# Row sums over single squares: the norm behind a down projection, with some of its additions moved to TensorE

## The chip, the cores and the metric

The kernel runs on one core of a Trainium2 chip. The metric is device time in microseconds (us). The kernel before took 2602.65 us, the median of three runs (2602.61 to 2605.37).

The engines are TensorE (PE; the profile shows its matmuls as PE and its weight loads as PEld), VectorE (DVE), ScalarE (ACT), GpSimd (POOL) and SyncE (SP), which here only issues DMAs. PE multiplies a stationary 128x128 block with a moving block and writes into PSUM banks of 512 float32 columns; DVE and ACT read the banks.

## The reference, cut to what matters

Two layers of a diffusion backbone run over 1024 latent tokens of width 1024, with a context of 256 tokens in front. Layer 0 mixes tokens by retention, layer 1 by a short gated convolution; each mixer is followed by a SwiGLU feed-forward network (FFN). Every sub-layer starts with an RMS norm over the 1024 features of a token, then a shift and a scale:

```
def rms_norm(x, gain=None):
    y = x * rsqrt(mean(x * x, axis=-1) + EPS)
    return y * gain

hx = hx + g1 * mixer(modulate(rms_norm(hx, norm_mix), sh1, sc1))
hx = hx + g2 * swiglu(modulate(rms_norm(hx, norm_ffn), sh2, sc2))
...
return rms_norm(hx, final_norm)
```

So four times a projection ends, a gated result is added to the residual stream, and the next thing that is needed is, per token, the sum of the squares of all 1024 features: after the retention output projection, after the first FFN, after the convolution's output projection and after the second FFN, where the norm makes the kernel's output.

## The kernel before, in words

The stream is held with features on partitions: eight tiles `H[kt, tb]` (kt 0 to 7) of 128 features by 512 tokens for each of the two halves of the tokens (tb). Matrix products are done in float32 by splitting both operands into a high and a low part: three matmuls for each block, in `mm3` (lines 160 to 162, the bulk of PE's work). The operands are made by a cast on ACT (L155, L150) and a subtraction on DVE (L156, L151). Large products use a Winograd-like scheme of seven sub-products, numbered 1 to 7, over a two by two division.

`down` (called four times) is the down projection. Its loop goes over sub-products in the order 1, 5, 6, 3, 7, 4, 2. Sub-products 3 and 7 finish the four upper and 4 and 2 the lower half of the work; 4 and 2 belong to the token half `order[0]`, 4 first (kt 4 to 7), then 2 (kt 0 to 3). For a finished tile, `finished` calls `update` (L1267: PSUM times gate plus residual, on DVE), and `complete`: ACT squares the tile, and `sq_add` (square L294, add L298 on DVE) adds the square to one running tile `accs[tb]`. ACT also stores the tile to DRAM (L1290) in the first three calls.

The last rows of sub-product 2 are done column by column (c = 0 to 3), so that tiles become final one after the other: over four rows in the retention output projection and the first FFN, over two rows in the convolution (`short`, with four rows in all). In the last call the tokens of sub-product 2 are also split in two (`LATER`), and the second 256 tokens come at the very end, one column after the other.

The norm follows as steps. `rstd` sums the squares over the partitions on PE: for each block of 128 tokens (j) the running tile is the stationary operand and one column of ones moves (L303); this leaves the sum of each token on its partition, one column of a PSUM bank for each block. Then come a scaling (L308) and an inverse square root by Newton steps, all small DVE operations (L166 to L178). `rstd_diag` puts the result on four diagonals (L321), and `spread` multiplies ones with them (L329), which makes a bank with the factor of each token in all partitions; the modulators (L1445 and ACT L1447, L1449) apply it, and what they give are operands of the next layer. The first sub-products of the next layer only need the other token half, whose norm runs during sub-product 2.

At the end of the kernel there is no spread: the finished tiles are scaled by the final gain (L1559), transposed on PE into banks of 128 tokens by 512 features (`result_turn`, L1553), and `result_end` multiplies each bank by the factor of its tokens, even banks on DVE (L1574), odd ones on ACT (L1572), and sends each piece of 256 KB out by a DMA on SP's queue (L1575). Feature half e = 1 goes first, then e = 0.

The order of the work on each engine is not the written one everywhere. Steps of the next layer are written between products by a list of hooks, and a planner in the framework then orders the instructions of each engine ahead of the run: of those that its own cost model has ready, the one written first. Two accesses to one PSUM bank stand in a fixed order wherever the planner sees a dependence. Tiles come from pools with a fixed number of buffers: `ttile` has 12, PSUM has 8 banks.

Of the kernel before, what the change touches and what calls it, by code (L numbers as in the profile page):

```python
# [14 lines left out]
AF = mybir.ActivationFunctionType  # L15
ALU = mybir.AluOpType

P = 128
# [3 lines left out]
TB = 512  # L22
# [30 lines left out]
def hybrid_kernel(ctx: ExitStack, tc: tile.TileContext, a: dict):  # L53
    nc = tc.nc
# [18 lines left out]
    def ttile():  # L73
        return tp.tile([P, 512], F32, tag="t", name="tt")
# [15 lines left out]
    def bank():  # L90
        return pp.tile([P, 512], F32, tag="p", name="ps")
# [32 lines left out]
    ones = const.tile([P, P], F32, name="ones")  # L124
# [4 lines left out]
    hooks = deque()  # L129
# [106 lines left out]
    def until(ready):  # L236
        while not ready():
            hooks.popleft()()
# [53 lines left out]
    def sq_add(acc, h, first, n=512, eng=nc.vector):  # L292
        s = acc if first else ttile()
        ins = nc.scalar.activation(s[:, :n], h, AF.Square)  # L294
        if eng is nc.gpsimd:
            tc.keep_in_program_order(ins)
        if not first:
            eng.tensor_tensor(acc[:, :n], acc[:, :n], s[:, :n], op=ALU.add)  # L298

    def rstd(acc, nb, ps):  # L300

        for j in range(nb):
            nc.tensor.matmul(  # L303
                ps[:, j : j + 1], acc[:, j * P : (j + 1) * P], ones[:, 0:1],
                start=True, stop=True,
            )
        v = sm.tile([P, 8], F32, tag="rs_v", name="rs_v")
        nc.vector.tensor_scalar(  # L308
            v[:, :nb], ps[:, :nb], 1.0 / D, EPS, op0=ALU.mult, op1=ALU.add
        )  # L310
        y = sm.tile([P, 8], F32, tag="rs_y", name="rs_y")
        rsqrt(y[:, :nb], v[:, :nb], nb)
        return y

    def rstd_diag(acc, n):

        nb = n // P
        y = rstd(acc, nb, bank())
        dg = ttile()
        for j in range(nb):  # L320
            nc.vector.tensor_scalar(  # L321
                dg[:, j * P : (j + 1) * P], ident, y[:, j : j + 1], None, op0=ALU.mult
            )
        return dg

    def spread(dg, n):

        rb = bank()
        nc.tensor.matmul(rb[:, :n], ones, dg[:, :n], start=True, stop=True)  # L329
        return rb  # L330
# [230 lines left out]
    acc = ttile()  # L561
# [4 lines left out]
    dg = rstd_diag(acc, CTX)  # L566
# [596 lines left out]
    last = 2 * len(T_ORDER) - 1  # L1163
# [27 lines left out]
    LATER = slice(0, TB // 2), slice(TB // 2, TB)  # L1191
# [4 lines left out]
    def down(src, nh, w, gate, residual, order, consume, then=(), last=False):  # L1196
# [3 lines left out]


        seq = [(n, i) for n in (1, 5, 6, 3, 7, 4, 2) for i in range(nh)]
        wr, ws, xl, xs, accs, made = {}, {}, {}, {}, {}, set()

        def w_load(k, half):
            if k not in wr:
# [59 lines left out]
                h, ps = H[kt, tb][:, t], ps[:, t]  # L1266
                nc.vector.scalar_tensor_tensor(h, ps, g, h, op0=ALU.mult, op1=ALU.add)  # L1267

        def norm_steps(tb):
            box = {}  # L1270

            def diag():
                box["dg"] = rstd_diag(accs[tb], TB)

            def bank_of(i, step):
                if i == 0:
                    box["rb"] = spread(box["dg"], TB)
                step(box["rb"])

            return [diag, nothing] + [lambda i=i, f=f: bank_of(i, f) for i, f in enumerate(consume(tb))]  # L1280

        def complete(kt, tb, t):
            h = H[kt, tb]
            if tb not in accs:
                accs[tb] = ttile()
                nc.scalar.activation(accs[tb], h, AF.Square)
            else:
                sq_add(accs[tb][:, t], h[:, t], False, t.stop - t.start)
            if not last:
                nc.scalar.dma_start(h_d[kt][tb], h)  # L1290

# [6 lines left out]
        short = nh == KT // 2  # L1298
# [8 lines left out]
        def step(ps, c, w, x, t, first, end):  # L1307
            k = slice(c * P, (c + 1) * P)
            mm3(ps[:, t], w[:, 0, k], w[:, 1, k], x[:, 0, t], x[:, 1, t], first, end, False)

        def run():
            banks, kept = {}, []
            by_column = 0 if last else min(4, nh // 2)

            def finished(n, c, ps, t):
                j, r = D_OUT[n]
                kt, tb = 4 * j + c, order[r]
                update(n, kt, tb, ps, t)
                if n in (3, 7, 2, 4):
                    complete(kt, tb, t)  # L1320
                if last and n in (2, 4):
                    result_tile(kt, t)

            for m, (n, i) in enumerate(seq):
                which = "A" if n in (1, 6, 7, 4) else "B"
                if i == 0:
                    if n == 7:
                        load_h()
                    if n == 5:
                        until(lambda: src(2, nh - 1) is not None)  # L1330
                    if n in (1, 5, 2):
                        banks[which] = [bank() for _ in range(4)]
                    if n == 4:
                        hooks.extend(then[:1])
                        hooks.extend(norm_steps(order[1]))
                        hooks.extend(then[1:])
                    if n == 2 and last:
                        hooks.extend(
                            lambda kt=kt: result_turn(kt, LATER[0]) for kt in range(4, KT)
                        )  # L1340
                if n == 1 and not short:
                    w_rest(i)
                if n == 6:
                    w_load(nh + i, 0)
                until(lambda: m in ws)
                operands(m + D_AHEAD)
                w, x = ws.pop(m), xs.pop(m)
                if n == 2 and i == nh - by_column - 1:
                    operands(m + D_AHEAD + 1)
                if n == 2 and i >= nh - by_column:  # L1350
                    kept.append((i, w, x))
                    if i < nh - 1:
                        continue
                    for c in range(4):
                        ps = banks[which][c]
                        for k, w, x in kept:
                            step(ps, c, w, x, TOKENS, k == 0, k == nh - 1)
                        finished(n, c, ps, TOKENS)
                        unit_done(2)
                    continue  # L1360
                t = TOKENS
                if last and n == 2:
                    kept.append((w, x))
                    t = LATER[0]
                for c in range(4):
                    step(banks[which][c], c, w, x, t, n in (1, 5, 2) and i == 0, i == nh - 1)
                if i == nh - 1:
                    for c in range(4):
                        finished(n, c, banks[which][c], t)
                unit_done(2 if n in (1, 2, 4) or nh == 4 else 1)  # L1370
            if last:
                flush()
                acc = accs[order[0]]
                for c in range(4):
                    ps = bank()
                    for i, (w, x) in enumerate(kept):
                        step(ps, c, w, x, LATER[1], i == 0, i == nh - 1)
                    finished(2, c, ps, LATER[1])
                    if c == 0:
                        for kt in range(4):  # L1380
                            result_turn(kt, LATER[0])
                        y = result_norm(acc, LATER[0])
                    if c == 1:
                        result_end(y, LATER[0])
                        for kt in range(4, KT):
                            result_turn(kt, LATER[1])
                    if c > 1:
                        result_turn(c - 2, LATER[1])
                y = result_norm(acc, LATER[1])
                for c in (2, 3):  # L1390
                    result_turn(c, LATER[1])
                result_end(y, LATER[1])
            else:
                hooks.extend(norm_steps(order[0]))

        return ahead, run

# [160 lines left out]
        h = H[kt, 1][:, t]  # L1558
        nc.scalar.activation(h, h, AF.Copy, scale=cols[:, C_FIN + kt : C_FIN + kt + 1])  # L1559

    def result_norm(acc, t):
        return rstd(acc[:, t], (t.stop - t.start) // P, bank())

    def result_end(y, t):

        t0 = t.start // P
        for e in (1, 0):
            for tt in range(t0, t.stop // P):
                r = ttile()
                ps, f = r_banks.pop((tt, e)), y[:, tt - t0 : tt - t0 + 1]  # L1570
                if tt % 2:
                    nc.scalar.activation(r, ps, AF.Copy, scale=f)  # L1572
                else:
                    nc.vector.tensor_scalar(r, ps, f, None, op0=ALU.mult)  # L1574
                nc.sync.dma_start(a["out"][tt * P : (tt + 1) * P, e * 512 : (e + 1) * 512], r)  # L1575


    def conv_tap(k, ft):
# [68 lines left out]
    for i, (r, _) in enumerate(seq):  # L1647
# [8 lines left out]
        if r is not None and r[1] == steps - 1:  # L1656
            h = r[0]
# [135 lines left out]
```

## Time and profile before

| what | value |
|---|---|
| median of three runs | 2602.65 us |
| the profiled execution | 2606.16 us |
| its span, first to last instruction | 2604.4 us |
| PE, PEld, DVE, ACT, POOL busy | 98%, 80%, 73%, 48%, 14% |
| mean granted clock of TensorE | 0.994 |
| chain of waits, share of PE | 85% |

The profile shows one execution. A row of a timeline gives start, duration, engine, line, operation, what it writes and reads and how often, and in brackets how long the engine had been idle and for what it waited. A row of the chain of waits gives start, duration and the instruction whose end released the next. A table of windows gives the busy time of PE, PEld, DVE, ACT and POOL in each stretch, with their counts in brackets, then the granted clock, the share of the DMA engines and GB/s.

### The profile page before, as it was taken

What the parts mean: (1) busy time and instruction counts of PE and PEld (TensorE: products, weight loads), DVE (VectorE), ACT (ScalarE), POOL (GpSimd) and SP (SyncE); (2) the same over time, 40 slices, a digit from 0 to 9 for tenths busy, and PEclk for the clock granted to TensorE, in tenths of its full rate; (3) what the DMA queues carried; (4) which work ended last, traced back from release to release, by engine and by line L of the source; (5) the groups of instructions that cost most, each with busy time, mean ns of one, the idle gap of its engine ahead of it and who ended that gap; (6) DMA issues with size and microseconds to landing.
All of it is one profiled execution on the core that took longest, in us unless ns stands there. A gap on an engine that the chain in (4) does not pass through costs nothing.

```text
span 2604.4 us, 33352 instructions
## 1 busy us (share of the span) xinstructions
PE 2552.3 (98%) x11444; PEld 2091.2 (80%) x11444; DVE 1914.1 (73%) x3366; ACT 1248.9 (48%) x2245; POOL 352.4 (14%) x441
## 2 busy tenths in 40 slices
PE   8999999999999999999999999999989999999998
PEld 4788888887777887888888888888768888888888
DVE  7886797765887778777875768877687666656766
ACT  6743333446766555433333545533465333334544
POOL 1102343002211202000002100200112100002100
PEclk9999999999999999999999999999999999999999
DMA  9456344764789946455557855432684333329723
GB/s 355 172 178 238 106 162 166 267 210 163 253 297 301 256 152 144 158 193 163 177 198 240 249 160 153 92 104 88 198 235 97 121 98 109 109 89 318 190 86 114
DMA packets 220106, 466.08 MB, mean 179 GB/s; under 512 B 23841, under 2 KB 53665, under 8 KB 219937
## 3 DMA queue, kind: packets, MB, share of 16 engines
q1 hardware_dynamic: 149808, 307.90, 36.2%
q0 software_dynamic: 39744, 101.74, 14.9%
q10 hardware_dynamic: 30384, 54.32, 5.7%
q8 instruction: 90, 1.47, 0.2%
q14 instruction: 80, 0.65, 0.1%
HBM read 331.22 MB, written 120.06 MB: 173 GB/s over the span
## 4 chain that ended last, share of the span: by engine, by line
PE 85%; DMA 5%; DVE 4%; issue 3%; ACT 2%; POOL 1%; SPq 0%; DVEq 0%; ACTq 0%; POOLq 0%
PE ps L160 28%; PE ps L162 28%; PE ps L161 28%; DVE u L156 2%; DMA raw<-in_ada_w 1%; DMA tt<-os_d 1%; DMA raw<-in_w_o 1%; PE ps L1049 1%; DMA tt<-x_d 1%; DMA u<-q_d 1%; DMA raw<-in_w 0%; ACT u L155 0%; DMA raw<-in_w_kc 0%; DMA t<-h_d 0%; PE ps L329 0%
## 5 line engine op out<-in xcount | busy, mean ns | idle before, releaser
L160 PE MATMUL ps<-u 128*128 128x512 f32 (+1 forms) x3492 | 1362.1, 391 | 18.2 <-DVE u L156 6.7
L161 PE MATMUL ps<-u 128*128 128x512 f32 (+1 forms) x3492 | 1354.5, 388 | 2.7 <-DVE u L156 2.7
L162 PE MATMUL ps<-u 128*128 128x512 f32 (+1 forms) x3492 | 1353.9, 388 | 0.0
L160 PEld LDWEIGHTS ps<-u 128*128 128x128 f32 x3492 | 658.3, 189 | 161.6 <-DVE u L156 6.2
L161 PEld LDWEIGHTS ps<-u 128*128 128x128 f32 x3492 | 658.9, 189 | 137.8 <-DVE u L156 4.4
L162 PEld LDWEIGHTS ps<-u 128*128 128x128 f32 x3492 | 658.5, 189 | 134.7 <-issue 0.7
L155 ACT CAST u<-raw 128x512 fp32r<-128x512 f32 (+1 forms) x634 | 387.6, 627 | 357.4 <-PE ps L162 201.3
L156 DVE TENSOR_TENSOR u<-raw,u 128x512 fp32r<-128x512 f32 (+1 forms) x634 | 451.7, 726 | 46.6 <-ACT u L155 45.4
L156 DVE TENSOR_TENSOR u<-tt,u 128x512 fp32r<-128x512 f32 x328 | 217.5, 686 | 111.4 <-ACT u L155 109.4
L155 ACT CAST u<-tt 128x512 fp32r<-128x512 f32 x328 | 194.6, 620 | 197.3 <-DMA tt<-x_d 85.4
L478 ACT COPY tt<-ps 128x512 f32<-128x512 f32 x192 | 112.8, 587 | 224.6 <-PE ps L162 220.8
L151 DVE SCALAR_TENSOR_TENSOR u<-raw,u 128x512 fp32r<-128x512 f32 x168 | 114.9, 687 | 65.1 <-ACT u L150 65.1
L150 ACT ACTIVATE u<-raw 128x512 fp32r<-128x512 f32 x168 | 105.2, 631 | 81.3 <-PE ps L162 69.6
L1407 POOL DMA_DIRECT2D x_d<-tt x52 | 28.3, 544 | 843.2 <-DVE tt L1420 744.0
L766 DVE SCALAR_TENSOR_TENSOR u<-ps,u 128x512 fp32r<-128x512 f32 x128 | 85.3, 686 | 38.0 <-ACT u L765 37.7
L491 DVE TENSOR_TENSOR tt<-tt,ps 128x512 f32<-128x512 f32 x64 | 43.7, 682 | 71.7 <-PE ps L162 71.7
L765 ACT ACTIVATE u<-ps 128x512 fp32r<-128x512 f32 x128 | 73.8, 598 | 33.6 <-PE ps L162 31.6
L485 DVE TENSOR_TENSOR tt<-tt,ps 128x512 f32<-128x512 f32 x64 | 43.8, 685 | 52.5 <-ACT tt L478 51.9
L1267 DVE SCALAR_TENSOR_TENSOR t<-ps,ada,t 128x512 f32<-128x512 f32 x48 | 33.9, 747 | 51.1 <-PE ps L162 48.2
L156 DVE TENSOR_TENSOR u<-t,u 128x512 fp32r<-128x512 f32 x78 | 52.7, 686 | 19.2 <-ACT u L155 18.6
L224 DVE SCALAR_TENSOR_TENSOR t<-t,c_row 128x512 f32<-128x512 f32 x88 | 57.5, 684 | 9.5 <-DMA t<-in_ada_t 9.5
L708 POOL TENSOR_TENSOR u<-t,u 128x512 fp32r<-128x512 f32 x24 | 32.2, 1344 | 223.4 <-DVE tt L1024 113.0
(184 smaller groups left out, 2132.4 us busy)
## 6 DMA issues: line engine op xcount, KB each, us to landing
raw<-in_w SPq DMA_DIRECT2D x88, 512.0 KB, 4.1
tt<-x_d SPq DMA_DIRECT2D x176, 256.0 KB, 4.0
t<-in_ada_t SPq DMA_DIRECT2D x88, 256.0 KB, 6.5
raw<-in_w SPq DMA_DIRECT2D x88, 256.0 KB, 6.1
x_d<-tt ACTq DMA_DIRECT2D x78, 256.0 KB, 2.6
raw<-in_w_v SPq DMA_DIRECT2D x36, 512.0 KB, 5.1
raw<-in_ada_t SPq DMA_DIRECT2D x36, 512.0 KB, 5.5
x_d<-tt POOLq DMA_DIRECT2D x52, 256.0 KB, 2.7
```

Of the source, the lines that this page charges most:

```text
L150: nc.scalar.activation(dst_hi, src, AF.Copy, scale=-1.0)
L151: nc.vector.scalar_tensor_tensor(dst_lo, src, -1.0, dst_hi.bitcast(F32), op0=ALU.mult, op1=ALU.subtract)
L155: nc.scalar.copy(dst_hi, src)
L156: nc.vector.tensor_sub(dst_lo, src, dst_hi.bitcast(F32))
L160: nc.tensor.matmul(ps, w_hi, x_lo, start=first, stop=False, **kw)
L161: nc.tensor.matmul(ps, w_lo, x_hi, start=False, stop=False, **kw)
L162: nc.tensor.matmul(ps, w_hi, x_hi, start=False, stop=last, **kw)
L224: nc.vector.scalar_tensor_tensor(w[e], w[e], 1.0, c_row[:, k], op0=ALU.mult, op1=ALU.mult, accum_out=sums[:, e, ct : ct + 1],)
L478: nc.scalar.copy(m[p, n], ps)
L485: nc.vector.tensor_add(t, t, banks[p, "c"])
L765: nc.scalar.activation(s[:, 0], st[d][m], AF.Copy, scale=f)
L766: nc.vector.scalar_tensor_tensor(s[:, 1], st[d][m], f, s[:, 0].bitcast(F32), op0=ALU.mult, op1=ALU.subtract,)
```

## The change

In `complete`, for tiles of sub-product 2, the square is no longer added to the running tile but kept in a tile of its own (the list `apart`): for c = 2 and 3 in the retention output projection and the first FFN, for all four c in the convolution, and for c = 3 of the last 256 tokens at the end. `rstd` takes these tiles and adds them up in PSUM: for each block of 128 tokens one matmul for the running tile and one for each tile apart, accumulated into the same column. In `result_end` the e = 1 pieces of the last 256 tokens are scaled and sent in two halves of 256 features.

```
-    def rstd(acc, nb, ps):
+    def rstd(acc, nb, ps, apart=()):
+        terms = [acc, *apart]
         for j in range(nb):
-            nc.tensor.matmul(
-                ps[:, j : j + 1], acc[:, j * P : (j + 1) * P], ones[:, 0:1],
-                start=True, stop=True,
-            )
+            for i, q in enumerate(terms):
+                nc.tensor.matmul(
+                    ps[:, j : j + 1], q[:, j * P : (j + 1) * P], ones[:, 0:1],
+                    start=i == 0, stop=i == len(terms) - 1,
+                )
...
-        def complete(kt, tb, t):
+        def complete(kt, tb, t, alone):
...
-                sq_add(accs[tb][:, t], h[:, t], False, t.stop - t.start)
+                n = t.stop - t.start
+                if alone:
+                    apart.append(ttile())
+                    nc.scalar.activation(apart[-1][:, :n], h[:, t], AF.Square)
+                else:
+                    sq_add(accs[tb][:, t], h[:, t], False, n)
...
                 if n in (3, 7, 2, 4):
-                    complete(kt, tb, t)
+                    alone = n == 2 and t != LATER[0] and c >= (3 if last else 0 if short else 2)
+                    complete(kt, tb, t, alone)
...
-                y = result_norm(acc, LATER[1])
+                y = result_norm(acc, LATER[1], apart)
...
-                hooks.extend(norm_steps(order[0]))
+                hooks.extend(norm_steps(order[0], apart))
...
-                if tt % 2:
-                    nc.scalar.activation(r, ps, AF.Copy, scale=f)
-                else:
-                    nc.vector.tensor_scalar(r, ps, f, None, op0=ALU.mult)
-                nc.sync.dma_start(a["out"][tt * P : (tt + 1) * P, e * 512 : (e + 1) * 512], r)
+                n = 2 if e and t == LATER[1] else 1
+                for k in range(n):
+                    w = slice(k * 512 // n, (k + 1) * 512 // n)
+                    if tt % 2:
+                        nc.scalar.activation(r[:, w], ps[:, w], AF.Copy, scale=f)
+                    else:
+                        nc.vector.tensor_scalar(r[:, w], ps[:, w], f, None, op0=ALU.mult)
+                    nc.sync.dma_start(
+                        a["out"][tt * P : (tt + 1) * P, e * 512 + w.start : e * 512 + w.stop],
+                        r[:, w],
+                    )
```

More of the change, by code (lines that the diff above doesn't have):

```diff
@@ L313, in rstd, with rstd_diag @@
         return y
-    def rstd_diag(acc, n):
+    def rstd_diag(acc, n, apart=()):
         nb = n // P
-        y = rstd(acc, nb, bank())
+        y = rstd(acc, nb, bank(), apart)
         dg = ttile()
@@ L1202, in down @@
         seq = [(n, i) for n in (1, 5, 6, 3, 7, 4, 2) for i in range(nh)]
-        wr, ws, xl, xs, accs, made = {}, {}, {}, {}, {}, set()
+        wr, ws, xl, xs, accs, made, apart = {}, {}, {}, {}, {}, set(), []
         def w_load(k, half):
@@ L1267, in update, with norm_steps @@
                 nc.vector.scalar_tensor_tensor(h, ps, g, h, op0=ALU.mult, op1=ALU.add)
-        def norm_steps(tb):
+        def norm_steps(tb, apart=()):
             box = {}
             def diag():
-                box["dg"] = rstd_diag(accs[tb], TB)
+                box["dg"] = rstd_diag(accs[tb], TB, apart)
             def bank_of(i, step):
@@ L1559, in result_tile, with result_norm @@
         nc.scalar.activation(h, h, AF.Copy, scale=cols[:, C_FIN + kt : C_FIN + kt + 1])
-    def result_norm(acc, t):
-        return rstd(acc[:, t], (t.stop - t.start) // P, bank())
+    def result_norm(acc, t, apart=()):
+        return rstd(acc[:, t], (t.stop - t.start) // P, bank(), apart)
     def result_end(y, t):
```

## The prediction, made before the changed kernel was run

> **What bounds the kernel now.** I read the page first, then the chain of waits at the places where a down projection hands over to what follows, then the busy time and the granted clock of single stretches.
>
> ```profile
> span 2604.4 us, 33352 instructions
> PE 2552.3 (98%) x11444; PEld 2091.2 (80%) x11444; DVE 1914.1 (73%) x3366; ACT 1248.9 (48%) x2245; POOL 352.4 (14%) x441
> ...
> PE 85%; DMA 5%; DVE 4%; issue 3%; ACT 2%; POOL 1%; SPq 0%; DVEq 0%; ACTq 0%; POOLq 0%
> ```
>
> TensorE (PE) is busy 98% of the span and holds 85% of the chain. Work added to PE therefore shows in the end unless it falls into one of PE's few gaps, and work taken from VectorE (DVE) shows only where PE waits for DVE. Those gaps stand at four places that the change touches: the end of the retention output projection (992 us), of the first FFN (1626), of the convolution (1950), and of the kernel (2594). At the first, the chain runs:
>
> ```profile
> 992.49 0.76 DVE tt L1267
> 993.33 0.64 ACT tt L294
> 993.99 0.70 DVE tt L298
> 994.74 1.19 PE ps L303 x8
> 995.93 0.64 PE ps L160
> ```
>
> Update of the last tile, its square, the add on DVE, then the row sums: four matmuls, each of two passes, hence x8. The timeline gives PE's idle time ahead of the sums here and, second, at the convolution:
>
> ```profile
> 994.74 1.19 PE L303 MATMUL ps<-ones,tt 128*128 128x1 f32 x8 [2.29 <-DVE tt L298]
> 1954.15 1.44 PE L303 MATMUL ps<-ones,tt 128*128 128x1 f32 x8 [3.30 <-DVE tt L298]
> ```
>
> So PE does nothing from 992.45, and there from 1950.85, until DVE's add is through. What that costs beside the wait is seen in stretches cut where the clock changes:
>
> ```profile
> 992.10:995.51 3.41, 1.12 (x9) 0.77 (x7) 1.44 (x2) 1.10 (x2) 0.00 (x0) 1.00 0.22 83
> 995.51:998.93 3.42, 3.42 (x11) 2.74 (x11) 2.55 (x16) 0.00 (x0) 0.00 (x0) 0.50 0.00 0
> 998.93:1002.34 3.41, 3.41 (x15) 2.45 (x14) 1.48 (x4) 1.00 (x2) 0.00 (x0) 1.00 0.00 0
> 1626.14:1629.55 3.41, 3.41 (x21) 2.94 (x20) 1.44 (x2) 1.22 (x2) 0.00 (x0) 1.00 0.20 77
> 1944.42:1947.84 3.42, 1.79 (x7) 0.93 (x5) 3.42 (x6) 3.02 (x6) 0.00 (x0) 1.00 0.69 156
> 1951.25:1954.66 3.41, 0.51 (x5) 0.51 (x5) 2.85 (x5) 2.52 (x5) 0.00 (x0) 1.00 0.41 154
> 1954.66:1958.08 3.42, 3.42 (x11) 2.92 (x12) 2.28 (x10) 0.00 (x0) 0.00 (x0) 0.50 0.00 0
> 1958.08:1961.49 3.41, 3.41 (x8) 2.31 (x7) 1.56 (x9) 0.53 (x1) 0.00 (x0) 0.50 0.00 0
> ```
>
> The first number behind the window is its length, the second PE's busy time, the third from the right the granted clock. The clock changes on a grid of 3.41 us: after one with PE busy 1.12 or 0.51 us the next has half the clock, after one with 1.79 us it has not. A half-clock stretch loses up to 1.7 us of PE work. At the convolution there are two in a row, although PE was busy throughout the first of them: the row sums stand at its start, for 0.9 us (until 1955.59, quoted below) as against 0.4 us in the stretch from 995.51 (until 995.93). I read this as: the sums, which move one column each, hardly count as work for the clock. Where the stretches begin relative to the program need not be the same in each run.
>
> **The change, place by place.** The price of a pass, with the clock full, comes from the first FFN's end:
>
> ```profile
> 1628.68 0.95 PE L303 MATMUL ps<-ones,tt 128*128 128x1 f32 x8
> 1629.49 0.49 PE L160 MATMUL ps<-u 128*128 128x512 f32 x1
> ...
> 1632.97 1.13 PE L329 MATMUL ps<-tt,ones 128*128 128x512 f32 x2 [0.46 <-DVE tt L321]
> ```
>
> Eight passes take 1629.49 − 1628.68 = 0.81 us, 0.10 us each; with the clock partly halved they take 1.19 us or 1.44 us (at 994.74 and 1954.15), so up to 0.18 each. With two tiles apart the row sums grow from 8 to 24 passes, with four apart to 40, at the very end from 4 to 8.
>
> No row shows in which order PE will run the new passes. The code writes them column block by column block, and within a block the ready sums first and the last tile's last. All write one bank, and I assume that the planner keeps them as written; then the first block's ready terms run early, but the other blocks' terms stand behind the last square. The bound on the other side, all ready terms run early, is the first rival.
>
> *Retention output projection* (two tiles apart). The last square ends at 993.97, so the sums can go on 0.7 us earlier than 994.74: −0.7. Four of the 24 passes fit into the wait, 20 follow it where 8 did: 12 × 0.10 = +1.2. The two removed adds free DVE, which nobody waits for. From 992.45 on PE now idles or runs sums until about 996.0, 3.5 us; the half clock at 995.51 would slow the last of them (a quarter of the 20 at 0.18 instead of 0.10: +0.4). Sum +0.9; bounds −0.7 (early terms) and +2.6 (one half-clock stretch more).
>
> *First FFN's end.* Here nothing is gained from the removed adds: PE was busy through the whole stretch from 1626.14 to 1629.55 (3.41 of 3.41 us), with the next layer's product until the sums began, so it never waited for L298. The 16 further passes are PE work: +1.6. What can take some of it back is the 0.46 us in which PE waits for the norm's diagonal at 1632.97, if the planner puts the sums into the middle of that product. I take +1.4; bounds +1.1 and +1.8. Twenty passes in a row are 2 us in which the clock may see little work, where 0.81 us did no harm: a half-clock stretch (1.7) with a chance of one in four, +0.4.
>
> *Convolution* (four tiles apart). Here DVE does bound:
>
> ```profile
> L298 DVE TENSOR_TENSOR tt<-tt 128x512 f32<-128x512 f32 x4 | 2.7, 676 | 0.0
> ...
> 1951.03 0.66 DVE tt L1267
> 1951.69 0.60 DVE tt L298
> 1952.82 0.68 DVE u L151
> 1953.50 0.61 DVE tt L298
> 1954.15 1.44 PE ps L303 x8
> 1955.59 0.64 PE ps L160
> ```
>
> All four adds between 1943 and 1954.2 are removed, and DVE has no idle time in front of them (0.0). Two stand ahead of the last update (2 × 0.60 = 1.2 us); from the last square's end (1952.3, one square of 0.64 after the update's 1951.69) to the sums were 1.8 us more. So the last square is there about 3.0 us before 1954.15, near 1951.2. Eight of the 40 passes fit in front of it, 32 follow where 8 did: 24 × 0.10 = +2.4 at full clock, +4.3 at 0.18. Net −0.6 to +1.3; as the clock halves at some point of this long thin stretch, +0.3.
>
> *End of the kernel.* One tile of 256 tokens apart, and the first two output pieces halved.
>
> ```profile
> 2594.57 0.42 ACT tt L294
> 2595.02 0.43 DVE tt L298
> 2595.50 0.62 PE ps L303 x4
> ...
> 2598.50 1.41 DVE L1574 TENSOR_SCALAR tt<-ps,rs_y 128x512 f32<-128x512 f32 x2
> 2599.26 1.79 SPq L1575 DMA_DIRECT2D out<-tt  x4
> ...
> 2601.00:2602.00 1.00, 0.00 (x0) 0.00 (x0) 0.00 (x0) 0.00 (x0) 0.00 (x0) 0.50 1.02 387
> DMA to landing us min/median/max: 2.0/2.4/2.7
> ```
>
> Without the add the sums can start at 2595.03, −0.47; two more passes stand behind the square, +0.2. Half a piece leaves DVE about 0.26 us sooner (an add of 128x256 takes 0.43 in the chain, one of 128x512 0.70), so the first issue falls at 2599.00 and not 2599.26. But SP then issues six times instead of four, 1.79 / 4 = 0.45 us apart: the last at 2599.00 + 5 × 0.45 = 2601.25 instead of 2599.26 + 3 × 0.45 = 2600.6. The DMA engines are full while the pieces go out (share 1.02, 387 GB/s), a 256 KB piece takes 0.68 us, and an unhindered one lands after 2.0 us, 1.3 of them before its data move. The fifth issue (2600.80) then lands at 2602.8 and the sixth 0.68 later, 2603.5; before, the last landed at 2600.6 + 2.7 = 2603.3. So +0.2 from the halves. Sum −0.1; bounds −0.7 (no loss at SP) and +0.3.
>
> **Sum.** +0.9 + 1.4 + 0.4 + 0.3 − 0.1 = +2.9 us. The profiled execution took 2606.16 us (its span and 1.76 around it), so 2609.1 for one like it. The median of the runs shown is 2602.65, 3.5 lower (two half-clock stretches fewer would be 3.4); on it, 2605.5.
>
> [...]
>
> **The rivals.** Ready terms first: if the planner moves all passes whose tile is ready ahead of the last square, 8 remain behind it at each handover. Retention −0.7; first FFN still +1.1, as PE has no gap there; convolution: 32 early passes (3.2 us) start when the product ends, about 0.6 us before 1950.85 since one add ahead of it is gone, and end near 1953.4, the last eight near 1954.3, −1.3 against 1955.59; end −0.3. Sum −1.2: 2601.4. For it speaks that the planner goes by what is ready; against it the common bank. Chance 0.18.
>
> Slower, by the clock: the sums read as idling, and the 2 to 3.2 us of them cost one half-clock stretch more at each of three handovers. It decides where a stretch holds less than about 1.8 us of products: 1.12 us tripped it, 1.79 did not. +2.9 − 0.4 + 3 × 1.7 = +7.6: 2610.2. For it speaks the second half-clock stretch at 1958.08; against it, that it must fall badly at all three. Chance 0.18.
>
> Faster: ready terms first, and with the shorter waits the half-clock stretches at 995.51, 1954.66 and 1958.08 go: −1.2 − 5.1 = −6.3: 2596.4. Against it, that the sums must then count as work. Chance 0.06.
>
> The halved pieces do not do what they are for, since the data path is full either way; that is within the forecast's end term. A further 0.06 is for the tiles apart holding buffers that the next layer's copies wait for; four tiles held 3 us longer would cost some 1 to 3 us, 2607.
>
> **How the numbers follow.** The forecast has 0.52. What a measurement tells from no change is 0.2%, 5.2 us: faster is below 2597.4, slower above 2607.9. Faster comes from the third rival: 0.06. Slower: most of the clock rival (0.14), a part of the forecast (0.05) and of the held buffers (0.02): 0.21. The rest, 0.73, is the same. The range takes in the ready-terms and the clock rival with half a stretch below the one and some tenths above the other: 2600.0 to 2610.5. The forecast's own range is 2603 to 2608.
>
> **What would show it.** L303 must have 24, 24 and 40 passes after 992, 1626 and 1950 us, and 8 at 2594, at 0.10 us each where the clock is full. The first product behind them comes at about 996.5 instead of 995.9, and at the first FFN the diagonal's spread (L329) 1.1 to 1.8 us later after the last update than before. The four L298 rows between 1943 and 1954 are gone. Six output DMAs end the kernel, the last issued 0.6 us later relative to the first scaling. The forecast is wrong if most sums run ahead of the last square, if half-clock stretches appear after 1630, or if the handovers' order on PE is another.

## The result and the profile after

The changed kernel took 2615.91 us, the median of five runs (2613.59 to 2618.87), beside 2602.94 us for the kernel before (2602.61 to 2606.23): a ratio of 1.0046, with a 95% interval of 1.0036 to 1.0057. A second comparison, ten runs beside 26, gave 2615.72 against 2605.24 us, ratio 1.0034 (1.0023 to 1.0045). So the change made the kernel slower by 0.3 to 0.5%. The prediction had said +2.9 us, which is no difference that can be told (chance 0.73), and had given a slower kernel a chance of 0.21.

The page of the changed kernel's profile, busy times and the chain by engine:

```profile
span 2614.1 us, 33483 instructions
PE 2561.6 (98%) x11512; PEld 2098.5 (80%) x11512; DVE 1907.7 (73%) x3358; ACT 1249.5 (48%) x2246; POOL 352.8 (13%) x441
...
PE 88%; DMA 5%; DVE 4%; issue 2%; ACT 1%; SPq 0%; POOL 0%; DVEq 0%; ACTq 0%; POOLq 0%
```

PE has 68 matmul passes more (11512 − 11444) and 9.3 us more busy time, DVE 6.4 us less; the span grew by 9.7 us. The saving on DVE is real and bought nothing; the span grew by about as much as PE's busy time. (Lines have moved: the sums are L306 now, the diagonals L324, the spread L332, squares kept apart L1294, updates L1270.)

The sums and the spread behind the retention, from the chain of waits (start and length in us):

```profile
993.06 2.14 PE ps L306 x20
...
998.53 2.08 PE ps L332 x2
```

and those of the first FFN and the convolution, from PE's timeline:

```profile
1630.53 2.73 PE L306 MATMUL ps<-ones,tt 128*128 128x1 f32 x24
1637.56 1.02 PE L332 MATMUL ps<-tt,ones 128*128 128x512 f32 x2
...
1950.33 0.57 PE L306 MATMUL ps<-ones,tt 128*128 128x1 f32 x4
1951.35 0.58 PE L306 MATMUL ps<-ones,tt 128*128 128x1 f32 x2
1956.80 0.42 PE L306 MATMUL ps<-ones,tt 128*128 128x1 f32 x2
1958.50 4.65 PE L306 MATMUL ps<-ones,tt 128*128 128x1 f32 x32
1967.92 2.07 PE L332 MATMUL ps<-tt,ones 128*128 128x512 f32 x2 [2.01 <-DVE tt L324]
```

The numbers of passes are those forecast: 24, 24, 40, in blocks of columns, with 20 and 32 of them together. The convolution is new: ACT's last square there started at 1953.18,

```profile
1953.18 0.63 ACT L1294 ACTIVATE tt<-tt 128x512 f32<-128x512 f32 x1 [0.33 <-DVE tt L1270]
```

and ended at 1953.81, but the 32 passes that need it run from 1958.50. The order on PE, which the planner sets ahead of the run, has a dozen matmuls of the next layer's product between them, and most of these ran at half the clock. (The second profile of the changed kernel has the same order, and there too the 32 passes start 3.7 us behind the square.) The windows show the clock (columns as in the prediction), cut at its own grid:

```profile
994.90:998.31 3.41, 1.54 (x8) 0.99 (x7) 2.67 (x16) 0.59 (x1) 0.00 (x0) 1.00 0.00 0
998.31:1001.72 3.41, 3.19 (x6) 1.87 (x7) 1.24 (x3) 0.29 (x1) 0.00 (x0) 0.50 0.02 5
1629.78:1633.19 3.41, 3.41 (x30) 3.25 (x28) 0.00 (x0) 0.59 (x1) 0.00 (x0) 1.00 0.19 67
1633.19:1636.60 3.41, 3.41 (x9) 2.68 (x9) 2.84 (x16) 0.00 (x0) 0.00 (x0) 0.50 0.00 0
1947.21:1950.63 3.42, 1.52 (x9) 0.98 (x8) 3.42 (x7) 3.14 (x6) 0.00 (x0) 1.00 0.80 171
1950.63:1954.04 3.41, 3.40 (x10) 2.62 (x10) 3.41 (x6) 3.05 (x6) 0.00 (x0) 0.50 0.44 165
1954.04:1957.45 3.41, 3.41 (x10) 2.76 (x10) 0.31 (x1) 0.70 (x2) 0.00 (x0) 0.50 0.19 73
1957.45:1960.87 3.42, 3.42 (x27) 3.20 (x27) 0.00 (x0) 1.74 (x4) 0.00 (x0) 1.00 0.02 5
1960.87:1964.28 3.41, 3.41 (x15) 3.22 (x15) 0.96 (x6) 0.00 (x0) 0.00 (x0) 0.50 0.00 0
1964.28:1967.69 3.41, 1.64 (x4) 0.72 (x3) 3.24 (x14) 0.59 (x1) 0.00 (x0) 0.50 0.00 0
1967.69:1971.11 3.42, 3.19 (x6) 1.86 (x7) 1.85 (x4) 0.29 (x1) 0.00 (x0) 0.50 0.00 0
```

and, of the kernel before, the two stretches of that grid at the first FFN, the first with its eight sums:

```profile
1626.98:1630.39 3.41, 3.41 (x21) 2.95 (x20) 1.32 (x5) 1.18 (x2) 0.00 (x0) 1.00 0.20 77
1630.39:1633.80 3.41, 2.95 (x13) 1.88 (x11) 2.22 (x13) 0.59 (x1) 0.00 (x0) 1.00 0.00 0
```

Two rows of the changed kernel decide the case. In 1629.78 to 1633.19 and in 1957.45 to 1960.87 PE is busy without a gap, mostly with sums, and in the stretch after each the clock is halved. At the first FFN the kernel before has no half-clock stretch; at the convolution there are five now, 1950.63 to 1957.45 and 1960.87 to 1971.11, where there were two from 1954.66 (a third, at 1941.01, stood before the tiles apart come into play).

The end of the kernel, first the chain of waits with the last square and the sums, then SP's timeline with the issue of the output pieces and the times from issue to landing:

```profile
2604.34 0.42 ACT tt L1294
2604.81 0.84 PE ps L306 x6
```

```profile
2608.58 2.79 SPq L1589 DMA_DIRECT2D out<-tt  x6
DMA to landing us min/median/max: 1.8/1.9/2.3
```

The sums follow the square at once, with six passes for four. SP issues six pieces in 2.79 us instead of four in 1.79. From the start of the last block product (L160) to the end of the span it takes 10.89 us, and 10.87 before.

### The profile page after: what moved, and what is told of

It reads as the page before. It is cut to its first block, busy times and chain, and to the rows that moved or that the text cites. A ratio compares the mean times of both kernels' runs of the same rounds, so it can differ in the third digit from the quotient of the medians.

```text
span 2614.1 us, 33483 instructions
## 1 busy us (share of the span) xinstructions
PE 2561.6 (98%) x11512; PEld 2098.5 (80%) x11512; DVE 1907.7 (73%) x3358; ACT 1249.5 (48%) x2246; POOL 352.8 (13%) x441
## 3 DMA queue, kind: packets, MB, share of 16 engines
q8 instruction: 91, 1.49, 0.2%
## 4 chain that ended last, share of the span: by engine, by line
PE 88%; DMA 5%; DVE 4%; issue 2%; ACT 1%; SPq 0%; POOL 0%; DVEq 0%; ACTq 0%; POOLq 0%
PE ps L160 29%; PE ps L161 28%; PE ps L162 28%; DMA tt<-x_d 2%; DVE u L156 1%; DMA raw<-in_w 1%; PE ps L306 1%; PE ps L264 1%; PE ps L1052 0%; PE ps L332 0%; ACT u L155 0%; DMA u<-q_d 0%; DMA tt<-g_d 0%; DMA u<-vp_d 0%; DMA tt<-os_d 0%
## 5 line engine op out<-in xcount | busy, mean ns | idle before, releaser
L160 PE MATMUL ps<-u 128*128 128x512 f32 (+1 forms) x3492 | 1362.3, 391 | 21.1 <-DVE u L156 9.7
L160 PEld LDWEIGHTS ps<-u 128*128 128x128 f32 x3492 | 658.2, 189 | 165.9 <-ACT u L155 9.7
L1270 DVE SCALAR_TENSOR_TENSOR t<-ps,ada,t 128x512 f32<-128x512 f32 x48 | 33.9, 747 | 52.4 <-PE ps L162 51.7
```

The costliest lines, as they stand in the source:

```text
L160: nc.tensor.matmul(ps, w_hi, x_lo, start=first, stop=False, **kw)
```

## Where the time came from, by stages

PE runs the same 3636 block products in nearly the same order in both kernels, so the start of the n-th first matmul of a block (L160) dates each stage. The table takes the time between two such starts and subtracts that of the profile before. It has the three handovers; stages ahead of the change are left out, and the larger ones between are named below. "Narrow" sums move one column, "wide" ones 128.

```
stage (block numbers)          retention  first FFN  convolution
                               1290-1320  2215-2240  2660-2690
changed kernel, first profile    +1.55      +2.64       +4.62
changed kernel, second profile   +1.63      +2.65       +2.73
retention and first FFN alone    +1.55      +1.79       +0.02
convolution alone                -0.03      -0.02       +2.19
end alone                        +1.61      -0.03       -1.48
wide sums, changed kernel        -0.10      +1.90       -1.27
zero terms, all adds kept        +3.40      +2.63       +6.25
last tile's sums only            -0.72       0.00       -4.55
wide sums, kernel before         +0.02      +0.09       -1.58
narrow, term by term             +2.97      +1.77       +6.27
wide, term by term               -1.49      +1.90       -2.21
wide, last tile of convolution   -0.01      +0.09       +0.98
32 columns, changed kernel       +1.67      +1.79       +1.96
```

Each row is one execution, and executions of the same program differ: the kernel with the end alone changed has retention and convolution as before in its program, and differs by +1.61 and −1.48 there. The half clock behind the changed kernel's retention began at 998.31 us in its first profile and at 996.6 in its second; I take a part of such differences to be where the clock's grid fell, which no run shows by itself. A single number of that size proves nothing by itself; the medians below count for more.

Some stages with no edit in them moved too: the wait for reloaded operands near 1422 us (+1.8 in the first profile of the changed kernel, +0.7 in its second, +2.1 with wide sums in the kernel before), the one near 2384 us (+1.4 and −1.4), and the stretches around 1850 (+1.2 and −3.0) and 1905 (−1.8 twice, +2.4 with wide sums in the kernel before). The first comes in both kernels, the others in the runs as a whole with either sign, so I take them as scatter. The order of SP's and POOL's DMAs, apart from the output pieces, is the same in both programs.

## The experiments

The edits are shown shortened; they are made to the changed kernel. Theory A is that of the prediction's sum: the added passes are PE time, and what counts is where they stand. Theory B is its second rival: long sums read as idling, and the clock halves behind them. Theory C was that a small shift sets off later waits. The kernel before, run beside each group, had medians of 2605.30, 2605.24 and 2605.66 us (31, 26 and 29 runs, 2597.74 to 2611.21 in all).

**Places alone: two tiles apart.**

```
-  c >= (3 if last else 0 if short else 2)
+  not short and not last and c >= 2        # and no halved pieces
```

> Only the two handovers with two tiles apart (retention output projection, first FFN); convolution and end as before. Theory A (the added passes are PE time at 0.115 us each, 32 of them, 3.7 us, less what the earlier square gives back at the first): +3 us over the kernel before, and no half-clock stretch beyond those of the kernel before. Theory B (long sums read as idling and halve the clock): +4 to +7 us, with a half-clock stretch right behind the sums of the first FFN, where the kernel before has none. Theory C (the time comes from later waits for reloaded operands near 1422 and 2392 us, which any shift sets off): those waits grow here too, by 1 to 2 us each.

2608.88 us, ratio 1.0019 (1.0004 to 1.0033). Both stages carry it, +1.55 and +1.79. In this execution the first FFN has no half-clock stretch; its sums:

```profile
1627.37 2.73 PE L306 MATMUL ps<-ones,tt 128*128 128x1 f32 x24
1633.45 1.12 PE L332 MATMUL ps<-tt,ones 128*128 128x512 f32 x2 [0.46 <-DVE tt L324]
```

and +1.79 is the bare price of 16 passes, 0.11 us each; PE still waits 0.46 us for the diagonals, so nothing is given back there. With the half-clock stretch (2.64, 2.65 in the changed kernel) 0.85 more. By medians the run is +3.6 us, which is theory A's +3 for this pair of places rather than theory B's +4 to +7. Theory C fails here: the stage near 1422 is unchanged.

**Places alone: the convolution.**

```
-  c >= (3 if last else 0 if short else 2)
+  short                                    # all four, only here; no halved pieces
```

> Only the convolution has its four tiles apart; the rest as before. Theory A: 32 more passes, 3.7 us, less up to 3 us for the four adds: about +1 us. Theory B: +4 to +6 us, with four or more half-clock stretches between 1940 and 1975 us against three before. Theory C: nothing before 1940, and the wait near 2392 us grows by 1 to 2 us.

2609.64 us, ratio 1.0012 (1.0001 to 1.0024). By medians that is +4.3 us, within theory B's +4 to +6 and not theory A's +1. The execution profiled is one of the shorter ones (2606.23 us); its stage is +2.19, with four half-clock stretches, at 1940.4 and three in a row from 1954.0, where theory B had four or more. The wait near 2384 did not grow.

**Places alone: the end.**

```
-  c >= (3 if last else 0 if short else 2)
+  last and c >= 3                          # halved pieces kept
```

> Only the end: one tile of 256 tokens apart and the halved first output pieces. All theories: between -0.4 and +0.3 us behind the last product, nothing ahead of it; the whole time the same as before within 1 us.

2605.22 us, ratio 1.0 (0.999 to 1.001), and 10.89 us behind the last product. As forecast, the end gains nothing and costs nothing. The three places together, +3.6, +4.3 and −0.1 by medians, make +7.8 of the 10.5 us by which the whole change's median lies above that of the kernel before in the second comparison.

**The same passes, wider.**

```
-  ps[:, j : j + 1], q[:, j * P : (j + 1) * P], ones[:, 0:1]
+  ps[:, j * P : (j + 1) * P], q[:, j * P : (j + 1) * P], ones
```

> The changed kernel with the row sums' moving operand 128 columns of ones instead of one (the same sums, 128 times over), so that each pass does real array work behind a weight load of the same length. Theory A: the passes cost what they cost, 0.115 us each, and the time stays at that of the changed kernel, 2614 to 2618 us. Theory B: the sums now count as work for the clock; the half-clock stretches behind the first FFN and in the row at the convolution go, and the time falls by 4 to 8 us, to 2608 to 2612.

(The scaling behind them then reads the first column of each block.) 2608.20 us, ratio 1.0009 (0.9996 to 1.0023), 7.5 us under the changed kernel's 2615.72 of the next group; the three stages of the table make 8.3 and 6.5 us of difference to the two profiles of the changed kernel. PE's order of matmuls is that of the changed kernel in all but 28 of 11,512 places, so it is not another order that makes the difference. Its windows at the convolution, and from PE's timeline the 32 passes there:

```profile
1949.82:1953.24 3.42, 3.42 (x19) 2.85 (x18) 3.10 (x6) 3.41 (x8) 0.00 (x0) 1.00 0.47 177
1953.24:1956.65 3.41, 3.41 (x28) 3.24 (x27) 1.28 (x2) 1.00 (x2) 0.00 (x0) 1.00 0.02 5
1956.65:1960.06 3.41, 2.10 (x15) 1.59 (x13) 1.95 (x10) 0.59 (x1) 0.00 (x0) 1.00 0.00 0
1960.06:1963.48 3.42, 1.83 (x6) 1.22 (x7) 2.06 (x9) 0.00 (x0) 0.00 (x0) 1.00 0.00 0
```

```profile
1954.10 3.73 PE L306 MATMUL ps<-ones,tt 128*128 128x128 f32 x32
```

This is the row to hold against 1957.45 to 1960.87 of the changed kernel: 28 matmuls where that has 27, as busy (3.41 us for 3.42), 27 loads in each (3.24 us and 3.20), and behind it the granted clock is 1.00 where it was 0.50 there. 32 wide passes take 3.73 us, 0.117 each; the same 32 narrow ones take 3.63 us at full clock in the second profile of the changed kernel, 0.113 each. So here a pass cost nearly the same with 1 and with 128 columns moving, and of these two stretches only the one with wide passes is followed by the full clock. Theory A is out as a whole account; its passes remain, +1.90 at the first FFN.

**The whole change again.** No edit.

> The changed kernel once more, beside the kernel before on the same chip: the scatter of single runs is some 3 us either way, and the first comparison had five of each. All theories: slower by 7 to 13 us. If it comes out under 5 us slower, the places alone (+3.6 and +4.3 us) add up and nothing is left that only the whole change has.

2615.72 us, ratio 1.0034 (1.0023 to 1.0045). This is above the 5 us below which the places alone would have accounted for all; 2.6 us by medians are left beside their sum, within the scatter of these runs. This profile has half-clock stretches at 996.6 (two), 1634.9, 1942.1, 1948.9 and 1962.6, so three at the convolution, as many as the kernel before. Its span, 2606.0, is 8 us under that of the first, more by the scatter around 1850 and 2384 than by the handovers.

**The passes without the gain.** All adds stay on DVE, and the running tile is multiplied with a column of zeros as often as there were tiles apart.

```
-  terms = [acc, *apart]
+  terms = [(acc, ones[:, 0:1])] + [(acc, zero_column)] * count
```

> The kernel before with all its VectorE adds, and the row sums lengthened to the changed kernel's numbers of passes (24, 24, 40 and 8) by matmuls of the running tile with a column of zeros; the sums stay the same. Theory A: 64 more passes behind the same waits, 7.4 us at 0.115 us each, and no more. Theory B: 7.4 us and three to five half-clock stretches more at the handovers, 1 to 1.7 us each: +10 to +15 us.

2619.43 us, ratio 1.0056 (1.0037 to 1.0075), +14.2 by medians, nearly twice the 7.8 us that its 68 passes more cost at 0.115 each. At the convolution the clock is halved for one stretch at 1949.6 and four in a row from 1959.8, and ten passes take more than 2 us there:

```profile
1961.06 0.59 PE L306 MATMUL ps<-ones,tt 128*128 128x1 f32 x2 [3.32 <-DVE tt L298]
1961.51 1.84 PE L306 MATMUL ps<-scz,tt 128*128 128x1 f32 x8
1963.21 0.56 PE L306 MATMUL ps<-ones,tt 128*128 128x1 f32 x2
```

From one block's start to the next are 2.15 us for ten passes, 0.21 each, beside 0.113 at full clock: in the halved clock the price was nearly doubled too.

**The gain without the passes.**

```
-  terms = [acc, *apart]
+  terms = apart[-1:] or [acc]
```

> The changed kernel with the row sums over the last tile apart alone, as many passes as before the change. It leaves out the squares of all other tiles at the four norms concerned, so it shows what the missing adds alone are worth. Both theories: retention -0.7 us, first FFN 0, convolution -2 to -4 us, end -0.4 us: 3 to 5 us faster than the kernel before.

2602.94 us, ratio 0.9987 (0.9975 to 0.9999). By medians that is 2.3 us faster than the kernel before, less than the 3 to 5 expected. The stages give −0.72 and 0.00, as both theories had them, and −4.55 where they had at most −4. At the convolution the sums are eight passes again and run directly behind a product:

```profile
1949.34 0.95 PE L306 MATMUL ps<-ones,tt 128*128 128x1 f32 x8
1955.07 1.13 PE L332 MATMUL ps<-tt,ones 128*128 128x512 f32 x2 [1.90 <-DVE tt L324]
```

No half-clock stretch follows. So the four adds are worth up to 4.6 us there, more than the 3.0 of the prediction, since with them two half-clock stretches go; in the changed kernel 32 more narrow passes, their place behind a product, and the clock cost more than that.

**Wide sums in the kernel before.** The edit of the wide sums, and no tile apart.

> The kernel before with row sums of 128 moving columns; all adds stay on VectorE. Theory A: no change within 1 us. Theory B: the sums keep the clock from halving a second time at the convolution and sometimes at the retention output projection: 1.5 to 4 us faster than the kernel before.

2600.66 us, ratio 0.9983 (0.9972 to 0.9995): 4.6 us faster than the kernel before by medians. The profile taken does not show where this comes from: it has as many half-clock stretches as the profile before, one at the retention handover (992.5) and three at the convolution (from 1944.8). They begin behind stretches in which PE mostly idles (busy for 1.12 and 1.02 us); but behind the convolution's sums the clock is full (1955.1), and that stage is 1.58 us shorter.

**Ready terms first.** All terms of one tile, then those of the next; one start of accumulation for the bank.

```
-  for j in range(nb):
-      for i, q in enumerate(terms):
+  for i, q in enumerate(terms):
+      for j in range(nb):
```

> The changed kernel with the sums written term by term and not block by block (one start of accumulation for the bank), so that only the last tile's eight passes stand behind its square; as many passes as in the changed kernel, of one column. Theory A (what costs is that 20 to 32 passes stand behind the last square): retention back to -0.5 us, convolution to about -2, first FFN still +1.8, in all within 1 us of the kernel before. Theory B (the number of thin passes and the clock cost, wherever they stand): 4 to 7 us slower than the kernel before, with half-clock stretches at all three handovers.

2614.41 us, ratio 1.0032 (1.0019 to 1.0044). As slow as the changed kernel: with narrow sums their order makes no difference that shows, and theory A's version of the loss fails again. Theory B had a half-clock stretch at all three handovers; the first FFN has none here. At the convolution the sums split into 16, 8, 8 and 8, with half-clock stretches at 1950.0 (three) and 1967.0 (two):

```profile
1950.08 3.41 PE L306 MATMUL ps<-ones,tt 128*128 128x1 f32 x16
1953.92 1.70 PE L306 MATMUL ps<-ones,tt 128*128 128x1 f32 x8
1960.28 0.95 PE L306 MATMUL ps<-ones,tt 128*128 128x1 f32 x8
1962.35 0.95 PE L306 MATMUL ps<-ones,tt 128*128 128x1 f32 x8
1968.07 2.08 PE L332 MATMUL ps<-tt,ones 128*128 128x512 f32 x2 [3.28 <-DVE tt L324]
```

The early passes cost 0.21 us each in the halved clock, which stays halved behind them.

**Ready terms first, and wide.** Both edits.

> Both at once: the sums term by term, each with 128 moving columns. Theory B: no half-clock stretch at the handovers and fewer passes behind the square; retention -0.7, first FFN +1.8, convolution -2 to -4: 1 to 3 us faster than the kernel before. Theory A: the same as the run with narrow columns term by term.

2604.60 us, ratio 0.9995 (0.9984 to 1.0005): 9.8 us below the narrow version of the same order, no half-clock stretch behind any handover, and stages of −1.49, +1.90 and −2.21, near those forecast. The whole was to be 1 to 3 us faster than the kernel before; it is 1.1 by medians, which the interval does not tell from nothing. So held at full clock the change gains nothing that shows; it moves 1.9 us onto the first FFN and takes 3.7 us off the other two. Beside the kernel before with wide sums (2600.66) it is 3.9 us slower by medians, though the intervals of the two ratios overlap: on these medians the better kernel is the one that widens the sums and leaves the adds on DVE.

**Wide, and one tile apart.**

```
-  c >= (3 if last else 0 if short else 2)
+  short and c == 3                         # wide sums, no halved pieces
```

> The kernel before with sums of 128 moving columns, and one tile alone apart: the last of the convolution, whose add waits longest on VectorE (eight more passes, 0.9 us, against 1.8 us). Theory B: 4 to 6 us faster than the kernel before, 0 to 1.5 faster than the wide sums alone. Theory A: 0 to 1 us faster than the kernel before.

2600.79 us, ratio 0.9985 (0.9973 to 0.9998): faster than both kernels, but not faster than the wide sums alone (2600.66). The one tile apart adds nothing that shows. Wide sums did not hold the clock where PE mostly idled: this profile has half-clock stretches at 993.1 and 1955.7, behind stretches with PE busy for 1.48 us, eight wide sums among it, and 0.99 us.

**32 columns.** The sums of the changed kernel with `ones[:, :32]`.

> The changed kernel with 32 moving columns in the sums. If the clock goes by the share of time in which columns move, a quarter of a full load does not hold it (the stretch with 1.79 of 3.41 us held, 1.12 did not), and the time is the changed kernel's, 2612 to 2617 us; if it goes by matmuls being issued at all, it would already hold in the changed kernel; if any wider operand is enough, 2606 to 2610 us as with 128 columns.

2611.23 us, ratio 1.003 (1.0013 to 1.0046), with half-clock stretches at 1000.3, 1942.4 and 1956.0 (three). By the median it lies between narrow and wide, and between the ranges expected for them; the intervals tell it from neither. The windows at the convolution show more:

```profile
1952.61:1956.02 3.41, 3.41 (x31) 3.41 (x31) 0.04 (x1) 0.64 (x2) 0.00 (x0) 1.00 0.02 5
1956.02:1959.43 3.41, 2.46 (x6) 1.35 (x5) 3.17 (x14) 0.58 (x1) 0.00 (x0) 0.50 0.00 0
```

28 of the first stretch's matmuls are sums of 32 columns, PE is busy throughout, and the clock is halved behind it: in this stretch a quarter of the columns did not hold it.

**The clock over all profiles.** The 14 profiles have 10,110 full-clock stretches of the grid between 100 and 2585 us. Counted in each are the columns of the moving operands of all matmuls that start in it; products alone make some 7,680. All 35 stretches with fewer than 2,560 columns are followed by half the clock, none of the 10,029 with 3,100 or more is, and of the 46 between 22 are. Seven of those followed by half the clock have 20 matmuls or more. So in these runs the clock went with the columns that moved, and neither with PE's busy time nor with the number of matmuls.

## Why the prediction was wrong

It gave +2.9 us and 2605.5; the comparisons gave +8.9 to +12 by their ratios. The step that failed is the clock's share in the sum: the forecast had read that the sums hardly count as work, and still charged one half-clock stretch more at 0.4 us, at the first FFN alone. The same passes with 128 columns took 7.5 us less by medians. A second step failed at the convolution, the place of the sums in PE's order. Point by point:

*The price of a pass, and the order.* Right. 0.10 us was forecast, 0.11 measured at full clock; the planner kept the blocks, and 20 and 32 passes stand behind the last square. The ready-terms rival (2601.4) fails as well: with that order written in, the run took 2614.41 us.

*Retention, +0.9.* It was +1.55 and +1.63. The 0.7 us that the add gives back are right (−0.72 in the run without the passes). The 20 passes took 2.14 us, 0.11 each, all at full clock, so the +0.4 for a quarter of them at half clock didn't come. Missed was what hangs behind them: PE had only a few matmuls left while the norm was made on DVE, was busy for 1.54 of 3.41 us in the stretch from 994.90, and the half clock then fell on the spread (2.08 us, where the first FFN's took 1.02).

*First FFN, +1.4 and +0.4 for the clock.* The first is +1.79, its upper bound: the 0.46 us wait was not used up. (The row from 1626.14 on which this rests is not cut on the clock's grid, whose edge is at 1626.98; PE is as busy there.) The second was a chance of one in four of 1.7 us. The clock halved in three of the six profiles with 24 sums of fewer than 128 columns there, with 0.85 us each time, and the traces show what differed: 24, 20 and 19 of the sums started in one stretch where it halved (both profiles of the whole change, and the zero terms), and they were split 11 and 13, 11 and 13, and 16 and 8 over two where it didn't (two tiles apart, term by term, 32 columns). A half-clock stretch behind 1630 was one of the prediction's own signs of being wrong.

*Convolution, +0.3.* It was +4.62 and +2.73, the largest miss, in two halves. That the sums run when the last square is there was wrong: the square ended at 1953.81 and the sums began at 1958.50, with a product in between in PE's order. And the thin stretch was priced by its passes (0.18 us at most), not by what the clock does to the products around it (0.43 us from one of their matmuls to the next at the half clock from 1954.04, 0.23 at the full clock from 1957.45). The zero terms show the price of the passes without the gain, +6.25 at the convolution, and the run without the passes the gain alone, −4.55. How much of the loss is the product in between was not tested by itself.

*End, −0.1.* Right: 10.89 us against 10.87 behind the last product. The halves land sooner each (median 1.9 us for 2.4), but SP issues six pieces for four.

*The clock rival, 2610.2, chance 0.18.* This is the nearest to what happened: the sums read as idling and cost time at half clock behind them, if not one stretch more at each handover in each run. What the prediction had in hand for it were the two stretches from 1954.66, with PE busy throughout and the clock still halved, and it read them so. Then it gave this reading 0.4 us at the first FFN, let it slow only the passes themselves elsewhere, and held against the rival that it must fall badly at all three places. The sums grew from about 0.8 us to 2 to 5 us of a 3.4 us grid; the count at the first FFN shows that this falls badly about every second time, not one time in four. The rival's boundary, 1.8 us of products, is only rough: a stretch with 1.57 us was followed by the full clock (1953.2 of the run without the passes), and one with 2.74 us, six sums among it, by half (1945.5 of the changed kernel's second profile).

*The level.* 2602.65 was the median of three runs. With 86 runs beside the experiments the kernel before has medians of 2605.2 to 2605.7 and single runs from 2597.7 to 2611.2. The forecast's range was built on the three, 2.6 to 3.1 us low. That is not what put it wrong: 8.9 us on 2602.65 are 2611.5, outside the range of 2600.0 to 2610.5 as well.

## What to carry to other kernels

Here a matmul with one moving column cost nearly as much as one with 128 (0.113 against 0.117 us), and a stretch in which PE was busy with them without a gap was followed by half the clock (1957.45, granted 0.50 behind it). Before moving sums to TensorE, count how many columns are left to move in a 3.4 us stretch (the boundary lay between 2,560 and 3,100 in these runs), or widen the sums, as in the runs with 128 columns. An add taken off a waiting engine is worth what stands in front of the wait in the order that the planner will make anew, not in the old one. And three runs that agree to 0.1% need not tell the level of a kernel whose single runs spread by 0.5%.

## What was not expected of the hardware

A stretch in which PE was busy for 3.42 of 3.42 us was followed by half the clock when most of its matmuls moved one column (1957.45), and a stretch busy for 3.41 of 3.41 us was not where they moved 128 (1953.24 of the wide run), at nearly the same price per pass, 0.113 against 0.117 us; 28 sums of 32 columns did not hold it (1952.61). Widening the sums of the kernel before, which adds work and removes none, made it 0.17% faster (0.05 to 0.28%). The scatter of one program, on one core of each of three chips, 2597.7 to 2611.2 us, is larger than most of the terms summed here. That it comes from where the clock's grid falls is likely from the stages (±1.6 us at handovers with the same program) but not shown; part of it stands near 1422, 1850, 1905 and 2384 us and was not followed further.
